# Moving the start of the row gathers, the last dots of one tile and its weighing across the end of a fused layer's front

## Chip, cores, metric

One core of a Trainium2 chip. The time is the device time of one execution in microseconds, the median over executions. The core has TensorE (PE, with its weight loads shown apart as PEld), VectorE (DVE), ScalarE (ACT), GpSimd (POOL) and SyncE (SP), each running its own stream of instructions in order; semaphores hold one engine until another, or a DMA, is done. DMAs are issued from the queues of SP, ACT and POOL and carried by 16 DMA engines. The granted clock that the profile shows for TensorE is a share of full speed, 1.00 at most.

## The reference, cut to what matters

One post-norm encoder layer over 1024 tokens of width 1024, float32. A projection feeds two mixers (forgetting attention and RWKV-7); their merge and a layer norm give x; then a PEER block adds, for each token and each of 8 heads, 16 experts out of 16384:

```python
q = (xb @ w_q).reshape(t, PEER_HEADS, 2, PEER_HALF)
s = jnp.einsum('thpd,hpkd->thpk', q, sub_keys)
top_s, top_i = lax.top_k(s, K)                       # K = 16 of 128, twice
...
best_s, best_pos = lax.top_k(cand_s.reshape(t, PEER_HEADS, K * K), K)
idx = jnp.take_along_axis(cand_i.reshape(t, PEER_HEADS, K * K), best_pos, axis=-1)
gate = jax.nn.softmax(best_s, axis=-1)
h = jax.nn.gelu(jnp.einsum('thkd,td->thk', u_table[idx], xb), approximate=False)
return jnp.einsum('thk,thkd->td', gate * h, v_table[idx])
```

So every token takes 128 rows of the table u (a dot with x each), a gelu, a gate, and a weighted sum of 128 rows of the table v. Then a second layer norm.

## The kernel before, in words

**Tiles.** The tokens are 8 tiles of 128. The *front* runs two halves of 512 tokens, each through `fox`, `rwkv_half`, `merge_half` and, at the end of the merge, `queries` (L1286): W_Q projections in sixteen column blocks, in four groups of four; each group's results are copied from PSUM to `q` on ACT (L1331) and scored against the keys `sk` (`scores`, called one group late), the scores are copied to `sc` (L1316) and stored from ACT's queue to the DRAM buffer `scd` (L1319).

**Experts two ways.** Tiles 3, 4 and 5 (`DENSE`) take all 16384 experts: their chosen experts and gates are turned into one-hot operands, multiplied on PE into a dense weight matrix, and u and v are read whole. Tiles 0, 1, 2, 6 (`GATHERED`) and 7 (`LAST`) gather. In `experts_in` (L1452) u's rows come one gather for a column of 128 indices (L1469, POOL) into a ring of places `g.keys`, and each is dotted with x on DVE (L1481, `tensor_tensor_reduce` into a column of `hh`); after 128 of them follow the gelu on ACT (L1486), the gate multiply on DVE (L1488) and a store to `cijd` in DRAM. The gate is loaded at the 65th dot, into a tile of its own. In the class `Rows`, v's rows are gathered in pairs (`gather`, L1852, POOL) and summed on PE (`pg<-vr,win`), with the weights placed by ACT into a window `win` of zeros.

**Background.** `topk` (L1346) and `experts_in` of all tiles form one background stream `g.B`, in the order k0, then each tile's experts mixed with the next tile's top-k: tile 0 with k1, tile 1 with k2, tile 2 with k3, then k4, k5, k6, tile 6 with k7, tile 7. Row sums form the stream `g.V`. Every matmul that goes through `mm` (L276) credits both with its modelled PE time multiplied by a rate; a dot costs 1.46 credits, a pair of rows 3. Rates by stage: `RATEP` for the three parts of the front, `RATEB` and `RATEV` later. `need(tag)` steps the stream until that part is done, whatever the credit.

**Order.** In the front PE's order is the program's and the other engines' is made when the program is built, by priorities, with background work high. In `dense_block` (from L1514) PE, POOL and DVE keep program order, and ACT and SP are ordered by priorities.

**The seam.** After the third group of projections `Rows.early` frees one of the `g.keys` places and loads into it tile 0's indices and weights and tile 3's selections (two POOL-queue DMAs). After the last projections `indices` turns both with six transposes on PE, copies them on ACT and makes the integer indices on DVE; then come the last scores. Then `begin(f"g2", "k3")` steps the background until tile 2's experts and tile 3's top-k are done; what is free of `g.keys` is lent as places and the first v rows are gathered. `vx` with `win` and the ring `vr`, `pp` with C (the dense weights) and, in `dense_block`, `bp` with the one-hot operands `ab` and `cT` are opened over the front's memory. A pool's first use waits for the release of everything that lay under it, unless the pool has `reuse_waits="tile"`, where each tile waits only for the tiles under itself.

**One-hot stage** (L1589 to L1630). k runs from −7 to 96, four tokens each. One-hots are made 3 steps ahead (`b` on DVE L1570, `a` on DVE L1576 or on ACT L1573, in turn), four products `v` go to PSUM, and two ACT copies move them: experts' first half to C (L1623), the rest to S (L1624), which is spilled every 8 steps (L1626, `cd<-S` on SP).

**Main loop** (L1730 on): for each j of 128, `usplit`, `hidden` (matmuls `b<-xh,uh`), `csplit` (a gelu on ACT, L1684, and multiplies with C), `vsplit` and `values`. u and v arrive by `uraw<-ut` and `vraw<-vt` on SP and are split into two fp32r parts by a cast on ACT and a subtraction (L293, L294). Ahead of the loop: two `usplit`, `hidden(0)`, `csplit(0)`, two steps of `g.V`, and two `vsplit`. Its pools are opened in the order `up` (raw u), `lp` (split parts, h), `rp` (raw v).

Of the kernel before, what the change touches and what calls it, by code (L numbers as in the profile page):

```python
# [23 lines left out]
BLEAD = 3  # L24
FIRST = 2.0
KRING = (5, 2)
TKW = (45.0, 56.25, 59.895)
TKI = 1
RATEP = (0.975, 0.975, 0.87)

# [373 lines left out]
def body(ctx, g):  # L404
# [36 lines left out]
    dve.tensor_copy(g.rank, g.iota[:, 0:16, None].to_broadcast([128, 16, 16]))  # L441
    g.scored, g.idx = set(), {}
    g.rows = Rows(g, GATHERED)
# [27 lines left out]
    with ExitStack() as fe:  # L471
        g.X = None
        setup = front_setup(g, fe, order)
        next(setup)
        for hf, (t0, n) in enumerate(PARTS):
            g.t0, g.n, g.cols = t0, n, slice(t0, t0 + n)
            with ExitStack() as hx:
                g.W.begin(hf, None if hf else hx.enter_context(tc.tile_pool(name="wr", bufs=1)))
                hp = hx.enter_context(tc.tile_pool(name="hp", bufs=1))
                kt = hp.tile([128, 4, n], F32, name="kt")  # L480
                more = [hp.tile([128, D], F32, name=f"g{i}") for i in range(KRING[1] if hf else 0)]
                g.keys.add(more)
                if g.X is None:
                    xload(g, hf, g.W._split)
                    next(setup)
                g.B.rate = RATEP[0]
                fox(g, hf, g.X)
                g.B.rate = RATEP[1]
                yr = rwkv_half(g, hf, g.X, kt) if g.stop != "fox" else None
                g.xs.close()  # L490
                g.X = None
                g.B.rate = RATEP[2]
                if g.stop not in ("fox", "rwkv"):
                    merge_half(g, hf, yr)
                g.keys.drop(more)
                g.B.busy = True
                while any(a is p for a in g.keys.alive.values() for p in more):
                    g.B._step()
                g.B.busy = False
    if g.stop:  # L500
        return
    g.rows.begin(f"g{SEL[-1] - 1}", f"k{DENSE[0]}")
    g.psB = ctx.enter_context(tc.tile_pool(name="psB", bufs=1, space=PSUM))
# [3 lines left out]
    g.spare, g.over = True, False  # L507
    g.rows.open()
    g.rows.places.add([g.vx.tile([128, D], F32, name=f"vr{i}") for i in range(RING)])
    g.V.add(g.rows.run())  # L510
    g.pp = ctx.enter_context(tc.tile_pool(name="pp", bufs=1))
# [774 lines left out]
def queries(g, hf, x1, rest, ps_):  # L1286
# [5 lines left out]
    with ExitStack() as fx:  # L1292
        qp = fx.enter_context(tc.tile_pool(name="qp", bufs=1))
        sk = qp.tile([128, 16, 128], F32, name="sk")
        sp.dma_start(sk, A["sk"])
        qs = {}

# [24 lines left out]
        for gr in range(4):  # L1322
# [12 lines left out]
            if gr == 1 and hf + 1 < len(PARTS):  # L1335
                xload(g, hf + 1)
            if gr == 2 and hf:
                g.rows.early()
        if hf:
            g.rows.indices(*[ps_.tile([128, 4, 128], F32, name=f"o{i}", bufs=2) for i in range(2)])  # L1340
        scores(*last)
# [112 lines left out]
def experts_in(g, tile_):  # L1454
# [17 lines left out]
    for k in range(128):  # L1472
        ahead()
        if k == 0:
            yield 1.0
            yield 1.0
        if k == 64:
            gate = P.tile([128, 128], F32, name="gate", bufs=1)
            sp.dma_start(gate, g.gated[tile_])
# [4 lines left out]
    if "hh" in g.dbg:  # L1484
        sp.dma_start(g.dbg["hh"][tile_ * 128:(tile_ + 1) * 128, :], hh)
    act.activation(hh, hh, AF.Gelu)  # L1486
    if tile_ != LAST:
        dve.tensor_mul(hh, hh, gate)  # L1488
        act.dma_start(g.cijd[tile_][:, 0, :], hh)
        yield 0.1  # L1490
        return
# [22 lines left out]
def dense_block(g, C):  # L1514
# [72 lines left out]
    lent = {1: g.rows.lent}  # L1587
    with tc.tile_pool(name="bp", bufs=BLEAD + 1) as bp, tc.tile_pool(name="cj", bufs=2) as cj:
        ab, pb = {}, {}  # L1589
        cT = bp.tile([128, 3, n - 128], F32, name="cT", bufs=1)  # L1590
        for k in range(-BLEAD - 4, n4 + 1):
# [13 lines left out]
            if 0 <= k < n4:  # L1605
                a, b = ab.pop(k)
                pb[k] = g.psV.tile([128, 4, 128], F32, name=f"v{k % 3}0")
                for u in range(4):
                    mm(g, pb[k][:, u, :], a[:, u, :], b[:, u, :], True, True)
            if k == n4 - XAT:  # L1610
                xp = zx.enter_context(tc.tile_pool(name="xp", bufs=1, side="right"))
# [21 lines left out]
    for q in range(UBUF):  # L1633
        uload(q)
    lp = lx.enter_context(tc.tile_pool(name="lp", bufs=2, reuse_waits="tile"))
    rp = lx.enter_context(tc.tile_pool(name="rp", bufs=VBUF, reuse_waits="tile"))
    for q in range(VBUF):
        load(q)

    def group(r):  # L1640
# [36 lines left out]
    def csplit(j):  # L1677

        if j < 128:
# [3 lines left out]
            h = lp.tile([128, n], F32, name="h")  # L1683
            act.activation(h, ph, AF.Gelu)  # L1684
            dve.tensor_mul(c, turned(h), c)
# [38 lines left out]
    g.V.busy = False  # L1724
    for q in range(2):
        vsplit(q)
    fin, old = iter(()), [p for j in range(LOOP, HALF - 7, 8) for i in range(nt) for p in parts(C, i, j, j + 8)]
# [34 lines left out]
class Rows:  # L1762
# [4 lines left out]
    def __init__(self, g, tiles):  # L1767
        self.g, self.tiles = g, tiles
        self.places, self.alive, self.meta, self.ng, self.pairs = Places(), [], {}, 0, False
        self.held = []  # L1770

    def open(self):

        self.win = self.g.vx.tile([128, 2, 159], F32, name="win")
        self.g.pool.memset(self.win, 0.0)

    def early(self):

        g = self.g
        kept, p = g.keys.all[:KRING[0]], None  # L1780
        g.B.busy = True
        while p is None:
            p = next((q for q in g.keys.free if any(q is a for a in kept)), None)
            if p is None:
                g.B._step()
        g.B.busy = False
        g.keys.free = [q for q in g.keys.free if q is not p]
        self.first = p
        g.pool.dma_start(p[:, 0:384].rearrange("p (a b) -> p a b", a=3), g.cijd[self.tiles[0]])
        g.B.need(f"k{DENSE[0]}")  # L1790
        g.pool.dma_start(p[:, 640:1024].rearrange("p (a b) -> p a b", a=3), g.cijd[DENSE[0]])

    def indices(self, pt, pd):

        g, p = self.g, self.first
        for j in range(3):
            g.pe.transpose(pd[:, j, :], p[:, 640 + 128 * j:768 + 128 * j], g.ident)
        cij = p[:, 0:384].rearrange("p (a b) -> p a b", a=3)
        for j in range(3):
            g.pe.transpose(pt[:, j, :], cij[:, j, :], g.ident)  # L1800
        self.meta[0] = self.turn(pt, cij, p[:, 384:512], p[:, 512:640].bitcast(I32))
        self.cT = p[:, 640:1024].rearrange("p (a b) -> p a b", a=3)
        g.act.copy(self.cT, pd[:, 0:3, :])
# [10 lines left out]
    def begin(self, *tags):  # L1814

        g = self.g
        for tag in tags:
            g.B.need(tag)
        self.lent = [g.keys.take() for _ in range(len(g.keys.free))]
        self.places.add(self.lent)  # L1820
        for _ in range(len(self.lent) // 2):
            self.gather()

# [21 lines left out]
    def gather(self):  # L1845
# [3 lines left out]
        for q in range(2):  # L1849
            place = self.places.take()  # L1850
            t = 64 * (k // 64) + 32 * q + k % 64 // 2
            g.pool.indirect_dma_start(out=place, out_offset=None, in_=g.A["v"], in_offset=bass.IndirectOffsetOnAxis(ap=self.meta[i][1][:, t:t + 1], axis=0))  # L1852
            self.alive.append(place)
        self.ng += 2

    def run(self):
        g, win = self.g, self.win
        prep = None
        for k in range(0, 128 * len(self.tiles), 2):
# [25 lines left out]
            if m == 31:  # L1885
# [4 lines left out]
                if s_:  # L1890
                    g.V.done.add(f"v{self.tiles[i]}")
                    if i == 0:
                        g.keys.give(self.first)
            del self.alive[:2]
# [135 lines left out]
```

## Time and profile before

| | us |
|---|---|
| median of 3 runs | 3493.19 (3491.34 to 3498.84) |
| profiled execution | 3488.81 |
| its span, first to last instruction | 3487.0 |
| busy PE | 3089.3 (89%) |
| busy DVE | 2376.6 (68%) |
| busy POOL | 1756.1 (50%) |
| busy ACT | 1140.0 (33%) |
| moved by DMA | 1132.22 MB, mean 325 GB/s |

The front ends about 1740 us into the span, the one-hot stage reaches to about 2180, the main loop to about 3455, and the last layer norms follow. Busy shares are averages over these stages. A row of the windows gives a stretch, its length, the busy time of PE, PEld, DVE, ACT and POOL with instruction counts, the granted clock, DMA's busy share (which can come out a little over 1) and GB/s. A row of a timeline gives the start, the busy time, the engine, the source line, the operation with output and inputs, and in brackets the idle time of the engine just before, with what ended it. A row of groups gives the count, the busy time and mean nanoseconds of one, then the idle time before them. DMA rows of the chain give the start and the time from issue to landing.

### The profile page before, as it was taken

The numbers are of one execution on the slowest core, as the hardware profiler recorded it, in microseconds if no ns is written. First come the engines' busy times: TensorE is split into PE (matmuls) and PEld (weight loads), VectorE is DVE, ScalarE is ACT, GpSimd is POOL, SyncE is SP. The second block draws the span as 40 slices with busy tenths as digits, with TensorE's granted clock in tenths as the row PEclk, the third lists the DMA queues.
The fourth block names the chain that finished last, engine by engine and source line by source line (L and its number), as shares of the span: only waits on it lengthen the run. The fifth ranks groups of instructions, "written<-read, shape, count | busy, mean of one in ns | idle before, by whom it ended". The sixth has DMA issues, their size and how long they took to land.

```text
span 3487.0 us, 54632 instructions
## 1 busy us (share of the span) xinstructions
PE 3089.3 (89%) x20141; PEld 2301.4 (66%) x20141; DVE 2376.6 (68%) x5489; ACT 1140.0 (33%) x2380; POOL 1756.1 (50%) x1430
## 2 busy tenths in 40 slices
PE   7899898999998878789777777999999999999996
PEld 5577776885566666567633332688887777777875
DVE  3234523358988898987479865687777767677776
ACT  3443223232432222111134443334333333333332
POOL 2032115325565456553464567555756566566761
PEclk9999999998998887989988989999999999999998
DMA  8373347889989778989998899999999999999995
GB/s 282 118 250 113 98 151 264 296 320 324 306 301 368 255 271 309 352 323 373 369 377 340 340 371 392 376 371 372 409 409 406 400 401 391 402 400 397 399 398 196
DMA packets 366876, 1132.22 MB, mean 325 GB/s; under 512 B 49456, under 2 KB 85936, under 8 KB 364816
## 3 DMA queue, kind: packets, MB, share of 16 engines
q0 software_dynamic: 184448, 671.56, 50.8%
q1 hardware_dynamic: 165760, 428.06, 33.7%
q10 hardware_dynamic: 16400, 29.11, 2.2%
q8 instruction: 158, 2.59, 0.3%
q14 instruction: 110, 0.90, 0.1%
HBM read 995.94 MB, written 132.64 MB: 324 GB/s over the span
## 4 chain that ended last, share of the span: by engine, by line
PE 47%; DVE 19%; DMA 16%; issue 7%; POOL 3%; ACT 2%; another core or an unknown queue 0%; SPq 0%; ACTq 0%; POOLq 0%; DVEq 0%
PE b L276 12%; PE v L276 10%; DMA uraw<-ut 8%; PE pj L276 7%; PE s L276 5%; PE o L276 5%; DVE g L1481 4%; PE pg L276 3%; DMA g<-u,idx 3%; PE S L276 2%; DVE ab L1570 1%; POOL g L1469 1%; DMA vr<-v,ve 1%; PE a L276 1%; DMA wl<-whd 1%
## 5 line engine op out<-in xcount | busy, mean ns | idle before, releaser
L1469 POOL DMA_INDIRECT g<-u,idx x569 | 685.3, 1204 | 609.0 <-DVE hh L1481 311.8
L1481 DVE CUSTOM_DVE_ANT_0 g<-g,ext 128x1024 f32<-128x1024 f32 x569 | 701.1, 1238 | 85.2 <-DMA g<-u,idx 66.8
L1852 POOL DMA_INDIRECT vr<-v,ve x285 | 338.1, 1186 | 174.0 <-PE pg L276 74.5
L276 PE MATMUL b<-xh,uh 128*128 128x384 f32 x1024 | 354.3, 346 | 41.0 <-ACT h L1684 39.7
L294 POOL TENSOR_TENSOR wl<-wraw,wh 128x1024 fp32r<-128x1024 f32 x63 | 152.7, 2424 | 436.7 <-ACT wh L293 337.2
L276 PE MATMUL b<-xl,uh 128*128 128x384 f32 x1024 | 352.1, 344 | 0.0
L276 PE MATMUL b<-xh,ul 128*128 128x384 f32 x1024 | 351.7, 343 | 0.1
L294 DVE TENSOR_TENSOR ul<-uraw,uh 128x512 fp32r<-128x512 f32 x256 | 176.0, 690 | 223.1 <-ACT uh L293 205.0
L276 PE MATMUL v<-vl,ch 128*128 128x512 f32 x768 | 301.9, 393 | 0.7 <-DVE vl L294 0.6
L276 PE MATMUL v<-vh,ch 128*128 128x512 f32 x768 | 301.1, 392 | 0.1
L276 PE MATMUL v<-vh,cl 128*128 128x512 f32 x768 | 300.9, 392 | 0.0
L276 PE MATMUL pj<-xh,wh 128*128 128x512 f32 x624 | 283.7, 455 | 13.9 <-ACT xh L293 7.1
L293 ACT CAST uh<-uraw 128x512 fp32r<-128x512 f32 x256 | 157.2, 620 | 410.2 <-PE b L276 210.0
L276 PE MATMUL pg<-vr,win 128*32 128x512 f32 x1364 | 243.2, 641 | 46.8 <-DMA vr<-v,ve 38.7
L276 PE MATMUL pj<-xl,wh 128*128 128x512 f32 x624 | 257.8, 413 | 2.4 <-DVE xl L294 2.4
L276 PE MATMUL pj<-xh,wl 128*128 128x512 f32 x624 | 257.5, 413 | 0.0
L276 PEld LDWEIGHTS b<-xh,uh 128*128 128x128 f32 x1024 | 196.3, 192 | 62.2 <-ACT h L1684 48.1
L276 PEld LDWEIGHTS v<-ab 128*128 128x128 f32 x768 | 111.1, 214 | 187.8 <-issue 113.4
L293 ACT CAST vh<-vraw 128x512 fp32r<-128x512 f32 x256 | 156.1, 618 | 162.1 <-PE v L276 115.5
L276 PEld LDWEIGHTS b<-xl,uh 128*128 128x128 f32 x1024 | 196.1, 192 | 15.2 <-issue 10.9
L276 PEld LDWEIGHTS b<-xh,ul 128*128 128x128 f32 x1024 | 195.9, 191 | 11.5 <-issue 9.8
L276 PE MATMUL v<-ab 128*128 128x128 f32 x768 | 139.8, 320 | 71.2 <-ACT S L1624 20.6
(395 smaller groups left out, 6555.2 us busy)
## 6 DMA issues: line engine op xcount, KB each, us to landing
uraw<-ut SPq DMA_DIRECT2D x128, 512.0 KB
vraw<-vt SPq DMA_DIRECT2D x128, 512.0 KB
wraw<-w SPq DMA_DIRECT2D x72, 512.0 KB
wh<-whd SPq DMA_DIRECT2D x72, 512.0 KB
wl<-whd SPq DMA_DIRECT2D x72, 512.0 KB
whd<-wh SPq DMA_DIRECT2D x71, 512.0 KB
whd<-wl SPq DMA_DIRECT2D x71, 512.0 KB
cd<-S SPq DMA_DIRECT2D x12, 1344.0 KB
```

The source lines that it names most:

```text
L276: g.pe.matmul(o, l, r, start=start, stop=stop_)
L293: g.act.copy(hi, src)
L294: (lo_eng or g.dve).tensor_sub(lo, src, hi.bitcast(F32))
L1469: pool.indirect_dma_start(out=place, out_offset=None, in_=A["uv"[n // 128]], in_offset=bass.IndirectOffsetOnAxis(ap=idx[:, n % 128:n % 128 ...
L1481: dve.tensor_tensor_reduce(out=gg, in0=gg, in1=xt, scale=1.0, scalar=0.0, op0=OP.mult, op1=OP.add, accum_out=hh[:, k:k + 1])
L1570: dve.tensor_scalar(b[:, u, :], g.iota, cT_[:, 2, t], cT_[:, 0, t], op0=OP.is_equal, op1=OP.mult)
L1852: g.pool.indirect_dma_start(out=place, out_offset=None, in_=g.A["v"], in_offset=bass.IndirectOffsetOnAxis(ap=self.meta[i][1][:, t:t + 1], ...
```

## The change

1. `RATEP[2]` 0.87 becomes 0.80; `KRING` (5, 2) becomes (6, 2), one more place for gathered rows for the whole front. `more`, the second half's two extra places, is dropped from the ring after the third group of projections.
2. `win` and a buffer of its own for what `early` loads (`p0`) move into the pool `g.gp`.
3. `early` runs at the start of the second `queries` and loads only tile 0's indices and weights, on ACT's queue. `indices` turns them in the first group. `coming` loads tile 3's selections after the third group (POOL's queue, after k3); `weights` turns them before the last scores.
4. `begin` asks for k3 alone. Three pairs of rows are gathered into `vr` places first, then the free `g.keys` places are lent and more pairs follow, ordered behind the first on POOL.
5. Tile 2's gelu, gate multiply and store become `weigh`, called in the one-hot stage once the dots are done and k is at least 4, with the gelu at that place in ACT's order.
6. In `experts_in` the gate is loaded at dot 126 and not 64, into the memory of the tile's indices (tile 7: of `t1`).
7. `bp` and `cj` get `reuse_waits="tile"`.
8. `rp` is opened ahead of `lp`; the casts of the first two `vsplit` are ordered behind the last gelu issued.
9. The scratch memory for POOL's DMA descriptors is 8192 bytes in place of the default 16384.

```diff
-KRING = (5, 2)
+KRING = (6, 2)
-RATEP = (0.975, 0.975, 0.87)
+RATEP = (0.975, 0.975, 0.8)
...
-    g.rows.begin(f"g{SEL[-1] - 1}", f"k{DENSE[0]}")
...
-    g.rows.open()
     g.rows.places.add([g.vx.tile([128, D], F32, name=f"vr{i}") for i in range(RING)])
+    g.rows.begin(f"k{DENSE[0]}")
...
         sp.dma_start(sk, A["sk"])
+        if hf:
+            g.rows.early()
...
+            if gr == 0 and hf:
+                g.rows.indices(ps_.tile([128, 4, 128], F32, name="o0", bufs=2))
             if gr == 2 and hf:
-                g.rows.early()
+                g.rows.coming()
+                g.keys.drop(g.more)
         if hf:
-            g.rows.indices(*[ps_.tile([128, 4, 128], F32, name=f"o{i}", bufs=2) for i in range(2)])
+            g.rows.weights(ps_.tile([128, 4, 128], F32, name="o0", bufs=2))
         scores(*last)
...
-        if k == 64:
-            gate = P.tile([128, 128], F32, name="gate", bufs=1)
+        if k == 126:
+            assert n >= 128
+            gate = g.tk.tile([128, 128], F32, name="t1") if tile_ == LAST else idx.bitcast(F32)
             sp.dma_start(gate, g.gated[tile_])
...
-    act.activation(hh, hh, AF.Gelu)
+    def weigh():
+        gelu = act.activation(hh, hh, AF.Gelu)
+        if tile_ == SEL[-1] - 1:
+            g.tc.keep_in_program_order(gelu)
+        if tile_ != LAST:
+            dve.tensor_mul(hh, hh, gate)
+            act.dma_start(g.cijd[tile_][:, 0, :], hh)
+    if tile_ == SEL[-1] - 1:
+        g.weigh = weigh
+        yield 0.1
+        return
+    weigh()
...
-    with tc.tile_pool(name="bp", bufs=BLEAD + 1) as bp, tc.tile_pool(name="cj", bufs=2) as cj:
+    with tc.tile_pool(name="bp", bufs=BLEAD + 1, reuse_waits="tile") as bp, tc.tile_pool(name="cj", bufs=2, reuse_waits="tile") as cj:
...
+            if g.weigh and k >= 4:
+                assert g.rows.ng < 128
+                g.weigh()
+                g.weigh = None
...
-    lp = lx.enter_context(tc.tile_pool(name="lp", bufs=2, reuse_waits="tile"))
     rp = lx.enter_context(tc.tile_pool(name="rp", bufs=VBUF, reuse_waits="tile"))
...
+    lp = lx.enter_context(tc.tile_pool(name="lp", bufs=2, reuse_waits="tile"))
...
-    for q in range(2):
-        vsplit(q)
+    with tc.issue_after(g.gelu.ins):
+        for q in range(2):
+            vsplit(q)
...
     def early(self):
...
-        g.B.need(f"k{DENSE[0]}")
-        g.pool.dma_start(p[:, 640:1024].rearrange("p (a b) -> p a b", a=3), g.cijd[DENSE[0]])
+        g.act.dma_start(self.first[:, 0:384].rearrange("p (a b) -> p a b", a=3), g.cijd[self.tiles[0]])
...
+    def coming(self):
+        g, p = self.g, self.first
+        g.B.need(f"k{DENSE[0]}")
+        g.pool.dma_start(p[:, 384:768].rearrange("p (a b) -> p a b", a=3), g.cijd[DENSE[0]])
...
-        self.lent = [g.keys.take() for _ in range(len(g.keys.free))]
+        for _ in range(len(self.places.free) // 2):
+            last = self.gather()
+        spare = len(g.keys.free)
+        self.lent = [g.keys.take() for _ in range(spare - (spare + len(self.places.free)) % 2)]
         self.places.add(self.lent)
-        for _ in range(len(self.lent) // 2):
-            self.gather()
+        with g.tc.issue_after(last.ins):
+            for _ in range(len(self.places.free) // 2):
+                self.gather()
...
-    nc = bacc.Bacc("TRN2", target_bir_lowering=False, num_devices=1)
+    nc = bacc.Bacc("TRN2", target_bir_lowering=False, num_devices=1, dynamic_dma_scratch_size=8192)
```

More of the change, by code (lines that the diff above doesn't have):

```diff
@@ L441, in body @@
     dve.tensor_copy(g.rank, g.iota[:, 0:16, None].to_broadcast([128, 16, 16]))
-    g.scored, g.idx = set(), {}
+    g.scored, g.idx, g.weigh = set(), {}, None
     g.rows = Rows(g, GATHERED)
@@ L482, in body @@
                 g.keys.add(more)
+                g.more = more
                 if g.X is None:
@@ L1485, in experts_in @@
         sp.dma_start(g.dbg["hh"][tile_ * 128:(tile_ + 1) * 128, :], hh)
-    act.activation(hh, hh, AF.Gelu)
+    def weigh():
[10 more added lines that the diff above has]
+    weigh()
     if tile_ != LAST:
-        dve.tensor_mul(hh, hh, gate)
-        act.dma_start(g.cijd[tile_][:, 0, :], hh)
         yield 0.1
@@ L1683, in csplit @@
             h = lp.tile([128, n], F32, name="h")
-            act.activation(h, ph, AF.Gelu)
+            g.gelu = act.activation(h, ph, AF.Gelu)
             dve.tensor_mul(c, turned(h), c)
@@ L1770, in __init__, with indices @@
         self.held = []
-    def open(self):
-        self.win = self.g.vx.tile([128, 2, 159], F32, name="win")
-        self.g.pool.memset(self.win, 0.0)
+        self.first = g.gp.tile([128, 768], F32, name="p0")
+        self.win = g.gp.tile([128, 2, 159], F32, name="win")
+        g.pool.memset(self.win, 0.0)
     def early(self):
         g = self.g
[L1780 to L1789, printed above, removed]
-        g.B.need(f"k{DENSE[0]}")
-        g.pool.dma_start(p[:, 640:1024].rearrange("p (a b) -> p a b", a=3), g.cijd[DENSE[0]])
-    def indices(self, pt, pd):
+        g.act.dma_start(self.first[:, 0:384].rearrange("p (a b) -> p a b", a=3), g.cijd[self.tiles[0]])
+    def indices(self, pt):
         g, p = self.g, self.first
-        for j in range(3):
-            g.pe.transpose(pd[:, j, :], p[:, 640 + 128 * j:768 + 128 * j], g.ident)
         cij = p[:, 0:384].rearrange("p (a b) -> p a b", a=3)
@@ L1800, in indices, with weights @@
             g.pe.transpose(pt[:, j, :], cij[:, j, :], g.ident)
-        self.meta[0] = self.turn(pt, cij, p[:, 384:512], p[:, 512:640].bitcast(I32))
-        self.cT = p[:, 640:1024].rearrange("p (a b) -> p a b", a=3)
+        self.meta[0] = self.turn(pt, cij, p[:, 0:128], p[:, 256:384].bitcast(I32))
+    def coming(self):
+        g, p = self.g, self.first
+        g.B.need(f"k{DENSE[0]}")
+        g.pool.dma_start(p[:, 384:768].rearrange("p (a b) -> p a b", a=3), g.cijd[DENSE[0]])
+    def weights(self, pd):
+        g, p = self.g, self.first
+        for j in range(3):
+            g.pe.transpose(pd[:, j, :], p[:, 384 + 128 * j:512 + 128 * j], g.ident)
+        self.cT = p[:, 384:768].rearrange("p (a b) -> p a b", a=3)
         g.act.copy(self.cT, pd[:, 0:3, :])
@@ L1851, in gather @@
             t = 64 * (k // 64) + 32 * q + k % 64 // 2
-            g.pool.indirect_dma_start(out=place, out_offset=None, in_=g.A["v"], in_offset=bass.IndirectOffsetOnAxis(ap=self.meta[i][1][:, t:t + 1], axis=0))
+            last = g.pool.indirect_dma_start(out=place, out_offset=None, in_=g.A["v"], in_offset=bass.IndirectOffsetOnAxis(ap=self.meta[i][1][:, t:t + 1], axis=0))
             self.alive.append(place)
         self.ng += 2
+        return last
     def run(self):
@@ L1891, in run @@
                     g.V.done.add(f"v{self.tiles[i]}")
-                    if i == 0:
-                        g.keys.give(self.first)
             del self.alive[:2]
```

## The prediction

> **What bounds the kernel now.** First the page's totals, its DMA row over 40 slices and the chain that ended last:
>
> ```profile
> span 3487.0 us, 54632 instructions
> DMA  8373347889989778989998899999999999999995
> PE 47%; DVE 19%; DMA 16%; issue 7%; POOL 3%; ACT 2%; another core or an unknown queue 0%; SPq 0%; ACTq 0%; POOLq 0%; DVEq 0%
> ```
>
> The profiled execution ran 3488.81 us (span 3487.0 and 1.8 outside it), 4.4 under the 3493.19 median of the runs; the sum is made against the former and 4.4 added at the end. TensorE carries half of the chain, and from the middle on DMA is full as well. Then the stretches around the seam that the change touches (start:end, us, busy of PE, PEld, DVE, ACT, POOL, then granted clock, DMA share, GB/s):
>
> ```profile
> 1697.00:1720.00 23.00, 21.32 (x115) 18.18 (x113) 13.97 (x23) 4.22 (x6) 11.51 (x12) 1.00 1.03 400
> 1720.00:1730.00 10.00, 0.27 (x1) 0.27 (x2) 7.79 (x15) 1.22 (x3) 2.22 (x3) 0.65 0.63 218
> 1730.00:1740.00 10.00, 5.03 (x30) 4.84 (x30) 0.52 (x2) 4.09 (x13) 5.83 (x7) 0.84 0.83 260
> 1740.00:1764.00 24.00, 9.92 (x47) 4.71 (x48) 6.08 (x21) 4.47 (x13) 15.88 (x17) 0.64 1.03 402
> 1764.00:2022.00 258.00, 190.40 (x1124) 90.46 (x1123) 230.10 (x1064) 118.02 (x388) 141.64 (x142) 0.85 0.91 343
> 2022.00:2178.00 156.00, 114.72 (x555) 45.41 (x554) 89.87 (x278) 54.03 (x179) 111.40 (x101) 0.90 1.01 393
> 2178.00:2202.00 24.00, 14.64 (x52) 7.36 (x53) 5.21 (x14) 7.17 (x15) 11.50 (x12) 0.69 1.02 411
> 2202.00:2670.00 468.00, 468.00 (x2511) 386.30 (x2511) 361.65 (x724) 179.39 (x359) 283.76 (x239) 1.00 1.01 388
> ```
>
> Up to 1718 the front projects, PE full. From 1720 to 1764 PE works 15.2 of 44 us. Then the one-hot stage: DVE sets its pace at first (230 of 258 us), DMA from 2022 on (1.01). From 2178 to 2202 PE works 14.6 of 24 us, and from 2202 the main loop holds it without a gap. Two holes, then, at the seams of the one-hot stage; what ends each stands in the timelines of PE, ACT and DVE (start, us, instruction, and in brackets the idle time before it and its releaser):
>
> ```profile
> 1729.73 5.30 PE L276 MATMUL o<-sk,q 128*128 128x128 f32 x30 [11.41 <-ACT q L1331]
> 1745.88 0.77 PE L276 MATMUL v<-ab 128*128 128x128 f32 x2 [10.85 <-DVE ab L1576]
> ...
> 2186.39 2.18 PE L276 MATMUL pg<-vr,win 128*32 128x512 f32 x8
> 2191.64 1.91 PE L276 MATMUL pg<-vr,win 128*32 128x512 f32 x2 [3.06 <-DMA vr<-v,ve]
> 2193.87 1.93 PE L276 MATMUL pg<-vr,win 128*32 128x512 f32 x6 [0.32 <-DMA vr<-v,ve]
> 2200.66 0.69 PE L276 MATMUL b<-xh,uh 128*128 128x384 f32 x1 [4.86 <-ACT h L1684]
> ```
> ```profile
> 1728.06 0.31 ACT L1486 ACTIVATE hh<-hh 128x128 f32<-128x128 f32 x1 [24.88 <-DVE hh L1481]
> 1729.09 1.56 ACT L1331 COPY q<-o 128x512 f32<-128x512 f32 x3 [0.72 <-DVE hh L1488]
> 1763.45 0.31 ACT L1623 COPY C<-v 128x176 f32<-128x176 f32 x1 [14.57 <-DMA C<-v,g]
> 2194.56 1.14 ACT L293 CAST vh<-vraw 128x512 fp32r<-128x512 f32 x2 [15.16 <-DMA vraw<-vt]
> 2198.82 1.28 ACT L1684 ACT_TABLE_LOAD   x1
> 2200.12 0.49 ACT L1684 ACTIVATE h<-b 128x384 f32<-128x384 f32 x1
> ```
> ```profile
> 1744.07 1.11 DVE L1570 TENSOR_SCALAR ab<-base,g 128x128 f32<-128x128 f32 x4 [12.00 <-DMA scd<-sc]
> 1745.10 0.68 DVE L1576 TENSOR_TENSOR ab<-base,g 128x512 f32<-128x512 f32 x1
> ...
> 1763.45 1.11 DVE L1570 TENSOR_SCALAR ab<-base,g 128x128 f32<-128x128 f32 x4 [13.85 <-remote]
> ```
>
> ACT stands 24.88 us at tile 2's gelu, which needs all 128 dots of that tile; the copies of the last three query projections are queued behind it, so PE waits 11.41 us for scores whose inputs are long in PSUM. The first one-hots then wait for the stores of those scores, and PE 10.85 more. A third hole follows, where DVE waits 13.85 us for something that the trace cannot name.
>
> **The change part by part, gain counted positive.** *Gelu moved* behind the fifth one-hot product: the copies go as soon as the projection ends.
>
> ```profile
> 1690.30 0.59 ACT L1331 COPY q<-o 128x512 f32<-128x512 f32 x1 [4.85 <-PE o L276]
> 1643.14 3.73 PE L276 MATMUL o<-sk,q 128*128 128x128 f32 x32
> ```
>
> Of 11.41 us one copy and its handover stay, 0.59 and some 0.3: +10.5. The scores then run without a long pause ahead of them, in the 3.73 us that 32 of them took at 1643 instead of 5.30 for 30: +1.5. *One-hot buffers that wait by tile*: they lie over the keys' half tiles and the queries, not over the scores' copies, so the last scores' matmuls free them, not the stores. What is left of 10.85 is one one-hot, 1.11 + 0.68 us, and a handover, 2 in all: +8.8. PE thus starts the stage at about 1725 instead of 1745.9. *The 13.85 us stall*: I know no cause, so it is taken to recur, 0. Its ends: all 13.85 gained, if the row gathers into C did it as the ACT row has it, and 10 lost, if the same gathers, now ahead of it, make it longer.
>
> *Dots moved into the one-hot stage.* The front's last rate falls from 0.87 to 0.80 credits per modelled PE us; by the cost model in the code the merge and the queries of the second half are 177.5 of those, so 12.4 credits, and at 1.46 a dot 8 dots of tile 2 are late. The dense stage runs them in program order on DVE, which paces it.
>
> ```profile
> L1481 DVE CUSTOM_DVE_ANT_0 g<-g,ext 128x1024 f32<-128x1024 f32 x384 | 475.9, 1248 | 76.9 <-DMA g<-u,idx 58.4 <-DMA cijd<-hh 9.1 <-issue 8.7
> L1570 DVE TENSOR_SCALAR ab<-base,cT 128x128 f32<-128x128 f32 x148 | 42.0, 361 | 0.5 <-issue 0.3 <-ACT cT L1560 0.2
> ```
>
> Eight by 1.248 are 10 us, the upper end if top-k falls behind by nothing. The credits are the same in number, so most dots put off steps of the next top-k to later, where DVE has room (362 of 468 us in the main loop); only that tile 4's must be done for the 25th one-hot forces some back: lower end 3. With the gate's load, now issued two dots before the end, DVE may stand a few us more, with the one-hots queued behind. I take 5: −5.
>
> *Row gathers first.* They begin when the indices are turned, with the last projections, and not after the gelu:
>
> ```profile
> 1721.20 0.94 POOL L1469 DMA_INDIRECT g<-u,idx  x1 [0.31 <-issue]
> 1732.34 0.95 POOL L1852 DMA_INDIRECT g<-v,g  x1 [9.82 <-DVE g L1811]
> L1852 POOL DMA_INDIRECT vr<-v,ve x285 | 338.1, 1186 | 174.0 <-PE pg L276 74.5
> ```
>
> POOL stands 9.82 us of that time. The new index load sits on ACT's queue, the three transposes, their copies and the two DVE steps go beside projections that PE is full of anyway: 0, and if that cover is gone, what the transposes take, under 1 us. The last u gathers of tile 2 come to stand behind 16 row gathers at about 1.25 us each on POOL, so until about 1740; the dots waiting for them come into the stage then, and their price is in the 5 above. *Scratch ring halved*: 0; if each gather took twice its 0.94, the first eight would come 8 us late. The Trainium skill, "SBUF — State Buffer", section "SBUF: two separate sides", has a VectorE operation in a two-port mode lock GpSimd out of writing a gather's descriptors, which would speak against more dots beside gathers; the gather at 1721.20 took its 0.94 us among dots end to end, so the sum leaves it at 0, where by the page it would be up to 10 us less.
>
> *End of the stage.* ACT casts V rows ahead of the first gelu, and those rows wait for the spill:
>
> ```profile
> 2178.38 9.14 DMA cd<-S
> 2187.54 6.94 DMA vraw<-vt
> ```
>
> The casts' 15.16 us wait then holds up the table load and the gelu that PE needs for its next group. In the change the casts come after that gelu, and the row buffers are laid out ahead of the split tiles, to lie over memory that is free earlier than the spilled tile. What is late next is PE's own work: two background steps that weigh gathered rows, in PE's order ahead of that group, the second waiting 3.06 us for its rows and ending at 2195.8. So of the hole PE's last 4.86 us go; the ends are 0 (DMA keeps the order of landings, and PE waits for V's rows a few matmuls later instead) and 9.5 (all up to 2191, where the rows have landed too). I take the row: +5.
>
> *Front.* One more place for gathered rows in the second half, against 58.4 us of DVE waits on them; 8% fewer dots there; the gate loads of tiles 0 and 1 later. From −17 (both gates uncovered, below) to +8; most rows say small: +2.
>
> *DMA must fit.* It stood empty 0.37 x 10 + 0.17 x 10 = 5.4 us from 1720 to 1740 and 0.09 x 258 = 23 us in the one-hot stage; later it has nothing free. So the gain fits, barely: I take 2 off.
>
> Sum: 10.5 + 1.5 + 8.8 − 5 + 0 + 5 + 2 − 2 = 20.8; 3488.8 − 20.8 = 3468.0 for a profile, and 3472 with 4.4 for the median.
>
> **Rivals.** *DMA takes the gain back*: the holes close, but the same bytes move at 1.01 share from 2022 to the end; only the 5.4 us of empty DMA are won, since the 9% of the one-hot stage are handovers that stay. 3493.2 − 5.4 = 3488. For it: the share row; against it: the main loop's first 468 us are bound by PE without a gap. The Trainium skill, "DMA: Bandwidth & Descriptors", section "Issuing engines are not separate DMA queues", speaks for this: transfers interleave on the same 16 engines whoever starts them, so that row gathers begun early would only push others back; the 1.03 at 1740 and 1.01 after 2022 agree, the 0.63 at 1720 does not.
>
> *The third hole goes too*: with the gathers 14 us earlier what DVE waits for has landed: 3472 − 13.85 = about 3458. For it: ACT's releaser is a row gather; against it: DVE's isn't named.
>
> *It doesn't do what it says*: if the first one-hots still lie over the scores' copies, 8.8 come back: about 3481.
>
> *Slower: gate loads hold DVE in the front.* Loaded at dot 126, a gate arrives after the last dot, and DVE, which bounds that stage, stands behind its multiply at tiles 0 and 1.
>
> ```profile
> 1775.65 9.20 DMA C<-cijd
> 1200.00:1300.00 100.00, 78.25 (x1000) 60.39 (x999) 95.34 (x254) 21.84 (x37) 55.15 (x46) 0.85 0.80 276
> ```
>
> A landing of 9.2 us twice is 18.4, decisive once no other DVE work is ahead of the multiply (DVE 95 of 100 us there); with DMA leaving only 5.4 of the gain, 3493.2 + 13 = 3506. Against it: the front's DVE order is made by a scheduler that can put other work ahead.
>
> **How the numbers follow.** Forecast 0.55, DMA takes it back 0.13, third hole gone 0.11, not as it says 0.11, slower 0.10. About 0.2%, 7 us, is what a measurement of this kernel can tell from no change: same is 3486 to 3500. Faster 0.55 + 0.11 + 0.11 = 0.77, same 0.13, slower 0.10. The forecast's own range, with the ends of the dots (3 to 10), the casts (0 to 9.5) and a front of −3 to +8, is 3458 to 3487: 2 + 4.5 + 6 better and the 2 of DMA, 5 + 5 + 5 worse. Below it, the third hole's case with some 8 of these is reached at 3450; above, the case of full DMA at 3488 with 3 for the front: 3491. What is left out is the slower case and the edges, 2 in 10.
>
> **What would show it.** In the profile after: PE's idle before the last 30 scores under 2 us, before the first one-hot product about 2; a row gather on POOL near 1718; dots among the one-hots on DVE, 8 of them, with waits on gathers or the gate of under 10 us together; the gelu of tile 2 without the 24.88; V's casts after the first gelu of the loop, PE's 4.86 us on ACT there gone; DMA's share in the one-hot stage near 0.97. Wrong if the one-hot stage, first product to last, grows by what the start gained, if DVE waits on a gate at tiles 0 and 1, or if POOL's gathers take longer than 1.19 us in the mean.

## The result, and the profile after

The changed kernel takes 3480.56 us in the median of 13 runs (3472.12 to 3491.77), and the kernel before took 3498.84 in the 13 beside them: a ratio of 0.995, 95% interval 0.9933 to 0.9967, so 17 us or 0.5% faster. 3472 had been forecast, inside 3450 to 3491. The profiled execution ran 3478.08 us, 10.7 under the one before. The page's totals and its chain:

```profile
span 3476.3 us, 54642 instructions
PE 52%; DVE 19%; DMA 12%; issue 6%; POOL 2%; ACT 2%; another core or an unknown queue 1%; SPq 0%; ACTq 0%; DVEq 0%; POOLq 0%
```

The same stretches as before:

```profile
1720.00:1730.00 10.00, 10.00 (x59) 4.45 (x52) 6.72 (x18) 4.46 (x17) 8.17 (x7) 0.88 1.03 409
1730.00:1740.00 10.00, 8.87 (x49) 3.47 (x50) 2.26 (x6) 3.06 (x10) 7.84 (x8) 1.00 0.99 381
1740.00:1764.00 24.00, 15.20 (x40) 4.79 (x34) 4.10 (x9) 4.12 (x14) 16.33 (x17) 0.70 0.98 371
1764.00:2022.00 258.00, 181.91 (x1084) 86.36 (x1084) 227.63 (x1056) 116.78 (x372) 131.00 (x133) 0.86 0.90 337
2022.00:2178.00 156.00, 111.72 (x520) 46.35 (x520) 81.46 (x249) 48.31 (x160) 109.34 (x101) 0.88 0.98 374
2178.00:2202.00 24.00, 17.93 (x80) 11.91 (x81) 12.89 (x30) 8.49 (x19) 9.66 (x10) 0.79 1.03 409
```

The seam of 1720 to 1740, where PE worked 5.3 us, now holds 18.9 us of PE and DMA is full in it. What stands there in the timelines of PE, ACT, DVE, POOL and SP:

```profile
1705.63 3.74 PE L276 MATMUL o<-sk,q 128*128 128x128 f32 x32
1711.55 0.46 PE L276 MATMUL v<-ab 128*128 128x128 f32 x2 [2.18 <-DVE ab L1593]
...
1771.69 0.77 PE L276 MATMUL v<-ab 128*128 128x128 f32 x2 [10.10 <-DVE ab L1587]
...
2183.41 1.91 PE L276 MATMUL pg<-vr,win 128*32 128x512 f32 x2 [5.91 <-DMA vr<-v,ve]
```
```profile
1759.92 0.19 ACT L1903 COPY win<-p 128x2 f32<-128x2 f32 x1 [9.16 <-remote]
...
1765.99 0.31 ACT L1494 ACTIVATE hh<-hh 128x128 f32<-128x128 f32 x1
...
2185.18 0.49 ACT L1705 ACTIVATE h<-b 128x384 f32<-128x384 f32 x1
2185.56 1.13 ACT L293 CAST vh<-vraw 128x512 fp32r<-128x512 f32 x2
```
```profile
1736.69 1.23 DVE L1487 CUSTOM_DVE_ANT_0 g<-g,ext 128x1024 f32<-128x1024 f32 x1 [8.11 <-DMA g<-u,idx]
1743.32 1.23 DVE L1487 CUSTOM_DVE_ANT_0 g<-g,ext 128x1024 f32<-128x1024 f32 x1 [4.36 <-DMA g<-u,idx]
1747.78 1.23 DVE L1487 CUSTOM_DVE_ANT_0 g<-g,ext 128x1024 f32<-128x1024 f32 x1 [1.60 <-DMA g<-u,idx]
1770.99 0.29 DVE L1498 TENSOR_TENSOR hh<-hh,idx 128x128 f32<-128x128 f32 x1 [21.98 <-DMA idx<-gated]
```
```profile
1706.89 0.94 POOL L1875 DMA_INDIRECT vr<-v,p  x1 [0.30 <-issue]
1730.94 0.95 POOL L1474 DMA_INDIRECT g<-u,idx  x1 [0.30 <-issue]
```
```profile
1761.56 0.32 SPq L1647 DMA_DIRECT2D cd<-S  x1
1762.22 0.30 SPq L1485 DMA_DIRECT2D idx<-gated  x1
```

The first hole is gone: the scores follow the projections at once and the first one-hot product 2.18 us after its predecessors. Two waits have taken its place, both on DVE among the one-hots. The last three dots of tile 2 wait 14.1 us for their rows, whose gathers come 24 us and more behind the first row gather on POOL. The gate multiply then waits 21.98 us, for two things. The gate's load may only overwrite the indices once the last gather that reads them has landed, and SP issues it behind the first spill of S, at 1762. And the multiply needs the gelu, which stands on ACT behind copies that wait themselves (one 9.16 us, for something that the trace cannot name) and ends at 1766.30. So only the last 4.7 us of the 21.98 belong to the gate's load alone. The one-hots behind that multiply are late, and PE 10.10 us with them.

To see where the 10.7 us are won and lost, the span is cut at events that both kernels have (starts in the timelines: first dot; first `o<-wh,mh` of the second half's merge; end of the last projection; first `v<-ab`; first and ninth `b<-xh,uh`; last one), here with all kernels of the experiments below, one profiled execution each. Executions of one kernel differ by some 10 to 30 us (e10 ran 3462 to 3491), so one row is one sample:

```
                 start   first dot  merge to   proj. to   one-hot   hidden 1  main   span
                 to dot  to merge   last proj. one-hots   stage     to 9      loop
before           797.1   757.3      163.0      28.5       433.0     21.8      1249.5 3487.0
after            792.6   747.5      165.4       6.0       459.1     17.2      1251.7 3476.3
e1  gate         798.0   750.2      165.3       6.9       444.7     17.1      1250.9 3469.8
e2  rate 0.87    800.8   751.0      181.3       5.8       445.9     18.0      1249.5 3489.1
e3  pool waits   793.0   746.6      163.3      16.0       438.6     18.6      1251.5 3464.4
e4  end          794.8   750.4      164.4       5.8       455.5     20.3      1248.3 3476.3
after, again     796.8   737.9      162.9       5.9       429.7     16.9      1252.6 3439.5
e5  place alone  789.1   733.3      163.3      27.9       408.4     21.7      1254.3 3434.9
e6  gate, 0.87   792.2   742.0      167.5       8.6       413.3     17.8      1251.5 3429.7
e7  gate, pool   791.9   735.4      164.7      15.5       419.4     17.1      1250.0 3430.8
e9  gate, 0.83   796.9   749.5      167.7       6.1       431.1     20.6      1250.2 3458.9
e10 gate again   791.6   747.0      165.3       7.0       446.7     17.1      1249.2 3460.6
e11 no place     797.4   758.2      163.4      11.2       442.3     19.3      1255.2 3483.8
e12 gate, 0.87   794.6   755.5      166.0       9.3       443.5     19.4      1255.4 3480.4
```

From the last hidden matmul to the end it is 36.7 to 36.9 us everywhere. After against before: −4.5, −9.8, +2.4, −22.5, +26.1, −4.6, +2.2. The first is scatter (789 to 801 in kernels alike up to there). So in these two executions the front, the start of the one-hot stage and its end gained 34.5 us between them, and the one-hot stage gave 26.1 back.

### The profile page after: what moved, and what is told of

Read it like the earlier page. It is cut to its first block, busy times and chain, and to the rows that moved or that the text cites. A ratio compares the mean times of both kernels' runs of the same rounds, so it can differ in the third digit from the quotient of the medians.

```text
span 3476.3 us, 54642 instructions
## 1 busy us (share of the span) xinstructions
PE 3087.4 (89%) x20141; PEld 2291.9 (66%) x20141; DVE 2375.7 (68%) x5489; ACT 1141.6 (33%) x2380; POOL 1760.3 (51%) x1429
## 4 chain that ended last, share of the span: by engine, by line
PE 52%; DVE 19%; DMA 12%; issue 6%; POOL 2%; ACT 2%; another core or an unknown queue 1%; SPq 0%; ACTq 0%; DVEq 0%; POOLq 0%
PE b L276 12%; PE v L276 12%; PE pj L276 7%; PE o L276 6%; DVE g L1487 5%; PE s L276 5%; PE pg L276 5%; DMA uraw<-ut 4%; DMA vr<-v,ve 3%; PE S L276 2%; DMA g<-u,idx 2%; DVE ab L1587 1%; DMA wl<-whd 1%; PE po L276 1%
## 5 line engine op out<-in xcount | busy, mean ns | idle before, releaser
L1474 POOL DMA_INDIRECT g<-u,idx x577 | 696.8, 1208 | 622.3 <-DVE hh L1487 313.5
L1487 DVE CUSTOM_DVE_ANT_0 g<-g,ext 128x1024 f32<-128x1024 f32 x577 | 710.7, 1239 | 98.9 <-DMA g<-u,idx 80.1
L276 PE MATMUL b<-xh,uh 128*128 128x384 f32 x1024 | 352.2, 344 | 36.4 <-ACT h L1705 32.8
L276 PE MATMUL pg<-vr,win 128*32 128x512 f32 x1420 | 276.3, 650 | 57.5 <-DMA vr<-v,ve 40.2
L276 PEld LDWEIGHTS b<-xh,ul 128*128 128x128 f32 x1024 | 194.8, 190 | 14.2 <-issue 9.6
L294 DVE TENSOR_TENSOR vl<-vraw,vh 128x512 fp32r<-128x512 f32 x256 | 176.1, 691 | 37.8 <-ACT vh L293 24.3
```

Of the source, the lines that this page charges most:

```text
L276: g.pe.matmul(o, l, r, start=start, stop=stop_)
L294: (lo_eng or g.dve).tensor_sub(lo, src, hi.bitcast(F32))
L1474: pool.indirect_dma_start(out=place, out_offset=None, in_=A["uv"[n // 128]], in_offset=bass.IndirectOffsetOnAxis(ap=idx[:, n % 128:n % 128 ...
L1487: dve.tensor_tensor_reduce(out=gg, in0=gg, in1=xt, scale=1.0, scalar=0.0, op0=OP.mult, op1=OP.add, accum_out=hh[:, k:k + 1])
```

## The experiments

The kernels of a group (e1 to e4; the changed kernel again with e5 to e7; e9 to e12) ran beside the kernel before on one chip; the chips differ (before took 3496, 3452 and 3498 us in the three groups), so ratios are compared within a group.

**e1, the gate early.** The gate of tile 2 goes into a part of p0 that is free once the indices are turned.

```diff
+        if k == 126 and tile_ == SEL[-1] - 1:
+            gate = g.rows.first[:, 128:256]
-        if k == 126:
+        elif k == 126:
...
     def coming(self):
+        g.sp.dma_start(p[:, 128:256], g.gated[SEL[-1] - 1])
```

> The changed kernel, but tile 2's gate is loaded from SP's queue with the last group of projections into a free part of p0, and no longer at dot 126 into the index tile. Theory A: the 21.98 us that DVE stands at tile 2's gate multiply, with the one-hots queued behind it, are most of what the one-hot stage lost, because the load stands on SP's queue behind the first spill. Then DVE waits under 3 us there, the copy to C of k = 8 comes some 18 us earlier than its 1766, the main loop's second group of hidden matmuls some 13 to 18 us earlier than its 2188, and the time is 0.990 to 0.992 of before. Rival B: the stage is paced by top-k of tile 4 and by DMA; the wait goes, k = 8 comes earlier, but by k = 28 (1865) the lead is gone and the time stays at 0.994 to 0.996.

3472.63 us, ratio 0.9934 (0.9909 to 0.9959). DVE no longer waits for the gate. But it still stood twice ahead of k = 8, here with the gelu on ACT:

```profile
1754.01 1.12 DVE L1589 TENSOR_SCALAR ab<-base,p 128x128 f32<-128x128 f32 x4 [11.77 <-remote]
1769.77 0.29 DVE L1500 TENSOR_TENSOR hh<-hh,p 128x128 f32<-128x128 f32 x1 [7.96 <-issue]
```
```profile
1769.42 0.31 ACT L1496 ACTIVATE hh<-hh 128x128 f32<-128x128 f32 x1
```

The first lies in a stretch in which PE goes on one instruction at a time with nothing to wait for (the third hole of the prediction). The second is the gelu's: the multiply starts when it ends. Theory A had put the whole 21.98 us down to the gate, but most of it was the gelu's in the changed kernel too. k = 8 came at 1770, not near 1748. The stage was 14.4 us shorter; the time lies between theory A and B and can't be told from the changed kernel's 0.995.

**e2, the rate back** (`RATEP[2]` 0.87).

> The changed kernel with RATEP[2] back at 0.87, so that the dots of tile 2 run in the front as before. Theory A: the front ended 12 us earlier because 7 dots (8.7 us) were taken out of a DVE that paces the merge and queries; then the last projection ends near 1715 to 1717 again and not at 1705, no dots stand among the one-hots, and the gate, loaded two dots before the end, has landed by the time it is needed: the time is 0.993 to 0.997. Rival B: the front's gain came from the added ring place; the last projection still ends near 1705 and the time is 0.989 to 0.992.

3492.51 us, ratio 0.9987 (0.9967 to 1.0007): nearly all of the gain gone, by a mechanism that neither theory had. The timelines of PE and SP:

```profile
1724.77 0.80 PE L276 MATMUL o<-xh,wh 128*128 128x512 f32 x1 [14.93 <-DMA wh<-whd]
```
```profile
1720.80 0.32 SPq L1485 DMA_DIRECT2D idx<-gated  x1
1721.23 0.37 SPq L324 DMA_DIRECT2D wh<-whd  x1
```

The gate's load waits on SP for the gathers that read the indices, and the weights of the last projection stand behind it. At the lower rate of the changed kernel the load comes after the projections, at 1762.

**e3, waits by pool** (`bp` and `cj` without `reuse_waits="tile"`).

> The changed kernel with the pools bp and cj waiting as before, for the release of everything under them. Theory A: PE's idle time ahead of the first one-hot product is 9 to 11 us again and not 2.18, and since DVE then stands for the gate anyway, only part of it reaches the end: 0.995 to 0.998. Rival B: all 8.8 us reach the end: 0.997 to 0.999. Rival C: the stores of the scores land while the row gathers hold DMA, so the wait is longer than before, 12 us or more, and the time 0.998 or above.

3473.99 us, ratio 0.9948 (0.9928 to 0.9967), level with the changed kernel's 0.995. The wait was there and did not reach the end; the stage itself came out 20.5 us shorter, in a profiled execution that is the quickest of its 12. The gate multiply waits 17.62 us here too, to the end of the gelu at 1763.64, with no part of it the gate's:

```profile
1718.88 0.77 PE L276 MATMUL v<-ab 128*128 128x128 f32 x2 [12.10 <-issue]
```
```profile
1763.68 0.29 DVE L1498 TENSOR_TENSOR hh<-hh,idx 128x128 f32<-128x128 f32 x1 [17.62 <-issue]
```

**e4, the end of the stage undone** (`lp` opened ahead of `rp`, the casts of V free).

> The changed kernel with lp opened ahead of rp again and the first casts of V free to go ahead of the first gelu. Theory A: that part was worth what the second group of hidden matmuls gained on the first, 21.7 us apart before and 17.3 after, so about 4.5 us: the two groups are 20 to 23 us apart again and the time is 0.996 to 0.997. Rival B: DMA's landings set that seam and the distance stays at 17 to 19 us, the time at 0.994 to 0.996.

3482.41 us, ratio 0.996 (0.9941 to 0.9978). The casts stand ahead of the gelu again and PE waits as it did before the change:

```profile
2191.15 0.69 PE L276 MATMUL b<-xh,uh 128*128 128x384 f32 x1 [4.97 <-ACT h L1705]
```

20.3 us between the two groups and not 17.2: 3 of the 4.6 us. In time, 0.996 can't be told from 0.995.

**The changed kernel again.**

> The changed kernel once more, beside the three below: 0.993 to 0.997 of before. Its second profile tells which of the stalls recur: if PE's slow steps near 1742 to 1760, one instruction each 0.7 us with nothing to wait for, belong to the program, they come again within 5 us of the same one-hots; if not, they move or go.

3439.97 us, ratio 0.9965 (0.9951 to 0.9979). PE's slow steps of 1742 to 1760 did not come; of DVE's two waits the rows' kept 14.2 us and the gate multiply's had 6.62:

```profile
1728.51 1.22 DVE L1487 CUSTOM_DVE_ANT_0 g<-g,ext 128x1024 f32<-128x1024 f32 x1 [8.51 <-DMA g<-u,idx]
1747.14 0.29 DVE L1498 TENSOR_TENSOR hh<-hh,idx 128x128 f32<-128x128 f32 x1 [6.62 <-DMA idx<-gated]
```

**e5, the ring place alone**, on the kernel before.

```diff
-KRING = (5, 2)
+KRING = (6, 2)
...
-    nc = bacc.Bacc("TRN2", target_bir_lowering=False, num_devices=1)
+    nc = bacc.Bacc("TRN2", target_bir_lowering=False, num_devices=1, dynamic_dma_scratch_size=8192)
```

> The kernel before with one thing of the change: one more ring place for gathered rows (KRING 6, 2), paid for by halved descriptor memory. Theory A: from the first dot to the last projection the changed kernel needs 913 us where before needs 920, with 747 to 751 against 757 already gone by at the merge, where the rate is the same, so the place is worth all of it: here too 913 and a time of 0.997 to 0.999. Rival B: the halved descriptor memory costs as much or the place hides nothing: 920 and 0.999 to 1.001.

3443.34 us, ratio 0.9978 (0.9966 to 0.999), where the whole change gave 0.9965. That is theory A's time. From the first dot to the last projection it takes 896.6 us where the changed kernel takes 900.8 on this chip, both far from the 913 and 920 of the first chip. So the place, with the smaller descriptor memory, is worth 0.22% (0.1 to 0.34). Its one-hot stage is 408.4 us beside 429.7 of the changed kernel on this chip: 21 us are lost there with no slow steps of PE in either.

**e6, gate early and rate 0.87.**

> The changed kernel with the gate loaded early into p0 and RATEP[2] back at 0.87. With the rate alone put back, the gate's load at dot 126 held SP's queue until the last gathers had landed, the weights of the last projections came late behind it, PE stood 14.93 us for them, and the time was 0.9987. Theory A: that queue was the whole loss; now the projections run through, the dots end with them, and the time is 0.991 to 0.995, as good as with the lower rate. Rival B: 7 dots in a DVE-paced front cost what they cost, 4 to 9 us more than with the rate of 0.80 (0.9934): 0.995 to 0.997.

3430.47 us, ratio 0.9942 (0.9921 to 0.9963), the best of this group: theory A, though the interval reaches into B. The projections run through (167.5 us and not 181.3), and the stage takes 413.3 us.

**e7, gate early, waits by pool.**

> The changed kernel with the gate loaded early into p0 and bp and cj waiting by pool. With the waits alone put back the time did not move (0.9948 against 0.995), PE standing 12.10 us ahead of the first one-hot product. Theory A: that was hidden behind DVE's wait for the gate; with the gate early it shows, 4 to 9 us: 0.995 to 0.997 where the early gate alone gave 0.9934. Rival B: the start of the one-hot stage isn't what its end hangs on; the time stays at 0.992 to 0.994.

3437.99 us, ratio 0.9964 (0.995 to 0.9978), level with the changed kernel's 0.9965. Against it the start is 9.6 us longer and the stage 10.3 shorter. Since the gate alone was not in this group, its 0.9934 of another chip can't be set beside this, so theory A is not excluded in time.

**e9, gate early and rate 0.83.**

> The changed kernel with the gate loaded early into p0 and RATEP[2] at 0.83: 3 dots of tile 2 are left for the one-hot stage, not 7, and all gathers of u's rows are issued ahead of the row gathers. Theory A: the price of the late dots is not their own time but that the gathers of the last three stand on POOL's queue and on DMA behind the row gathers, DVE waiting 14 to 22 us for them (22.3 of group g<-u,idx in the second profile of the changed kernel); here that wait is under 6 us, from the first one-hot product to the first hidden matmul 410 to 418 us go by, and the time is 0.991 to 0.994. Rival B: the dots' own time and the top-k steps put off set the stage, so 3 dots cost 3 sevenths: 0.994 to 0.996.

3459.12 us, ratio 0.9884 (0.9859 to 0.9909): 1.2% faster than before, the best kernel of all, and quicker than either theory had it. On POOL the last gather of u's rows is issued ahead of the first row gather, and none of the dots among the one-hots waits:

```profile
1715.40 0.94 POOL L1474 DMA_INDIRECT g<-u,idx  x1 [0.31 <-PE o L276]
1716.65 0.94 POOL L1878 DMA_INDIRECT vr<-v,p  x1 [0.30 <-issue]
```
```profile
1723.68 1.21 DVE L1489 CUSTOM_DVE_ANT_0 g<-g,ext 128x1024 f32<-128x1024 f32 x1
1733.48 1.22 DVE L1489 CUSTOM_DVE_ANT_0 g<-g,ext 128x1024 f32<-128x1024 f32 x1
1752.20 1.21 DVE L1489 CUSTOM_DVE_ANT_0 g<-g,ext 128x1024 f32<-128x1024 f32 x1
```

The stage took 431.1 us and not 410 to 418; PE's slow steps were there.

**e10, gate early and rate 0.80, in the same group.**

> The changed kernel with the gate loaded early into p0 and the rate of 0.80, beside the two rates above it. Theory A: the gate alone takes away the smaller wait only, 7 to 22 us by chip and execution; DVE's wait for the last three u rows stays at 14 to 22 us, and the time is 0.994 to 0.9965, behind both other rates. Rival B: the gate is all: 0.992 to 0.994, level with them.

3476.33 us, ratio 0.9939 (0.9918 to 0.996): 17 us behind 0.83, so not level with it, but level with 0.87 (e12): neither theory as it stands, and the number lies on the border of their ranges. Its profiled execution, with a span of 3460.6, is its quickest, and in it the dots did not wait for rows either, where theory A had 14 to 22 us. So the times show that 0.83 is better here, and the profiles do not show in which wait.

**e11, the change without the place** (`KRING` (5, 2)).

> The changed kernel with KRING back at (5, 2): the seam's parts without the ring place. Theory A: the place alone gave 0.9978 where the whole change gave 0.9965, so what remains of the change is worth 0.1 to 0.2%: 0.998 to 1.0. Rival B: the parts do not add, and the seam alone gives 0.995 to 0.997.

3486.87 us, ratio 0.9976 (0.996 to 0.9993). From the first dot to the merge it takes 758.2 us again, and all the seam's parts together are worth 0.24%, between the two theories. With e5's 0.22% they make 0.46%, where the whole change gave 0.5% on one chip and 0.35% on another. The intervals are too wide to say more than that the parts may add.

**e12, gate early and rate 0.87, in the same group.**

> The changed kernel with the gate loaded early and RATEP[2] at 0.87, once more for the comparison of three rates on one chip. Theory A: no dot and no gather is left, the front is 4 to 6 us longer than at 0.83: 0.993 to 0.996, not ahead of 0.83. Rival B: any dot in the one-hot stage costs more than in the front: 0.991 to 0.994 and ahead of both other rates.

3478.53 us, ratio 0.994 (0.9919 to 0.9962): as before for this kernel, and theory A. The rate of 0.83 is ahead of both neighbours, by intervals that do not meet, on this one chip.

## Why the prediction was right, and where it was not

The time lies in the range. A gain of 20.8 us was forecast, 17 was measured between the medians and 10.7 between the two profiled executions. But the mechanism was right in part only, and luck had its share: the range was 41 us wide, and half of the gain came from elsewhere. The seam's parts, 18.8 us of the forecast, are worth about 8 (e11: 0.24%); the ring place, priced at 2 us with all else in the front, about 8 as well (e5: 0.22%).

*Start of the one-hot stage*: 10.5 + 1.5 + 8.8 = 20.8 forecast, 22.5 measured (28.5 to 6.0). Right, and its parts too: PE's wait for the copies is nothing, the scores take 3.74 us, and e3 and e7 put the waits by tile at 10.0 and 9.6. **The step that failed** is the next one, that this start carries through to the end for a price of 5 us. In e3 and e7 the 10 us that the start lost came back from the stage, and the time did not move beyond its interval of some 0.2%. The stage grew by 26.1, more than the start had gained: the first of the prediction's own signs of being wrong.

*Dots in the one-hot stage*: −5, with an upper end of 10, for a stage that grew by 26.1. There are 7 of them, not 8. The term priced their own 1.248 us and had most of the top-k steps that they put off done later, where DVE has room. These steps were done in the stage, as the windows from the first one-hot product to k = 8 and from k = 16 to 28 show (starts of ACT's copies `C<-v`), before and after:

```profile
1745.90:1791.50 45.60, 34.62 (x176) 15.02 (x177) 30.85 (x147) 16.52 (x54) 28.11 (x29) 0.77 0.99 388
1832.40:1866.90 34.50, 29.42 (x180) 14.49 (x181) 32.81 (x133) 22.63 (x74) 14.36 (x14) 0.81 0.93 359
```
```profile
1711.50:1766.20 54.70, 40.13 (x160) 14.94 (x160) 19.09 (x50) 16.47 (x52) 40.73 (x38) 0.76 1.00 386
1811.80:1864.80 53.00, 33.71 (x207) 16.67 (x207) 47.78 (x216) 26.50 (x82) 23.33 (x24) 0.84 0.88 320
```

To k = 8, DVE is busy 19 of 54.7 us, with no top-k step done; from 16 to 28 it works off what was put off (216 instructions and 47.8 us, against 133 and 32.8), since tile 4's must be ready. The same measure in every profile, from the copy of k = 16 to that of k = 32, shows what this costs (late dots are those of tile 2 that stand among the one-hots):

| late dots | kernels | us from k = 16 to k = 32 |
|---|---|---|
| 0 | before, e2, e5, e6, e12 | 51.8 to 54.0 |
| 3 | e9 | 61.0 |
| 7 | after (twice), e1, e3, e4, e7, e10, e11 | 62.9 to 72.7 |

In e1 and e10 no late dot waited for its row, and they take 65.6 and 67.3 us. So this part is the work put off and not the waits. It is 12.8 of the 26.1 us (65.9 against 53.1). The other 13.7 fall ahead of k = 16 (100.2 against 86.5), where DVE's two waits and PE's slow steps lie; how these share them is not shown. From k = 32 on the two kernels take the same 293 us.

The gate's load had been put at "a few us more", and that holds. The multiply's waits read 21.98 and 6.62 us in the two profiles, but the gelu ended only 4.7 and 5.1 us ahead of it; the rest is the wait for the gelu, for which the sum had no term.

*Front*: +2 forecast, 7.4 measured (9.8 and −2.4). Groups of dots in the front, before and after:

```profile
L1481 DVE CUSTOM_DVE_ANT_0 g<-g,ext 128x1024 f32<-128x1024 f32 x376 | 466.1, 1248 | 76.2 <-DMA g<-u,idx 58.1 <-DMA cijd<-hh 9.1 <-issue 8.7
```
```profile
L1487 DVE CUSTOM_DVE_ANT_0 g<-g,ext 128x1024 f32<-128x1024 f32 x377 | 467.5, 1250 | 67.4 <-DMA g<-u,idx 57.9 <-DMA cijd<-hh 8.1 <-issue 1.0
```

DVE's idle time falls by 8.8 us; e5, with the place alone, has 66.0 of it, and e11, without the place, 75.4. The prediction looked at the 58 us on gathers, which did not move; the 8.7 on "issue" went. The lower rate, which the term also counted, wins nothing that shows: but for e2, merge to last projection is 163 to 168 us at 0.80, 0.83 and 0.87.

*End of the stage*: +5 forecast, 4.6 measured, with the releaser that was named: e4 brings the 4.97 us on ACT back. It is not always as much: with the change in place the two groups are 16.9 to 18.6 us apart in most kernels, but 19.3 to 20.6 in e9, e11 and e12; why is not shown.

*Third hole*: taken to recur, and it did here. In the kernel before PE goes one instruction at a time from 1753 to 1765, while DVE stands its 13.85 us. It does not belong to these instructions: none of the four kernels of the second group has a stretch of 8 us of it there, nor has e3, and in the third group it is there again. What makes PE take 0.7 us and more for each instruction stays open.

*DMA must fit*: from the first one-hot product to the first hidden matmul DMA's share was 0.95 before and 0.94 after, not 0.97. *Of the rivals*, slower by gate loads in the front is out: from the 128th dot to the multiply it takes 3.5 us in both kernels at tile 0 (1081.5 to 1085.0, 1075.3 to 1078.8), at tile 1 3.0 and 4.4 us. The mechanism was real at tile 2 instead, and through SP's queue (e2), which the rival did not name. DMA taking it all back is out in time (5.4 us, where the interval is 11 to 23); that the first one-hots wait as before is out, by PE's 2.18 us.

*Gathers beside dots*: 0, read off the gather at 1721.20 with its 0.94 us. That row was a lucky one: it began 0.13 us before its dot ended. A gather that begins earlier in a dot ends 0.8 us after that dot, as this one of the kernel before, and its dot:

```profile
1716.46 1.89 POOL L1469 DMA_INDIRECT g<-u,idx  x1 [0.30 <-issue]
```
```profile
1716.31 1.23 DVE L1481 CUSTOM_DVE_ANT_0 g<-g,ext 128x1024 f32<-128x1024 f32 x1 [1.06 <-DMA g<-u,idx]
```

Of 268 gathers there that begin 0.15 us or more before the end of a dot, 257 end 0.79 to 0.83 us after it; the 166 that run with no DVE instruction beside them take 0.94 us in the median and never more than 1.15. The 0 holds in size all the same: the gathers of u's rows take 1.20 us in the mean before and 1.21 after. The Trainium skill, "SBUF — State Buffer", section "SBUF: two separate sides", has a VectorE operation in a two-port mode lock GpSimd out; the trace agrees in the lock, and no run shows in which mode the dot runs.

*Transfers pushed back*: the late rows landed within 5.8 to 6.3 us of their gathers' issue (1730.94 to 1736.69, the first of them). What made them late was their place among the row gathers on POOL, and the gate's load stood behind the spill on SP. The Trainium skill, "DMA: Bandwidth & Descriptors", section "Issuing engines are not separate DMA queues", has transfers interleave whoever starts them; DMA's share of 0.98 to 1.03 from 1720 to 1764 agrees that the engines were full, but the two delays shown came from the order of issue.

## What to carry to other kernels

When work is moved past a seam, price what it puts off in its new place, before its own duration: 7 dots of 1.25 us made the stretch from k = 16 to 32 some 9 to 21 us longer, because the steps that they put off were due there. Where a wait has two releasers, look at the one that would have come next: the gelu alone held the multiply for 17 of the 22 us that the profile puts down to the gate. A load into memory that others still read holds up its whole queue (14.93 us of PE in e2), so give it memory that is free. A rate of 0.83 with the gate loaded early gave 1.2% where the change gave 0.5% and 0.35% on other chips; it leaves 3 late dots and issues the last gathers of u's rows ahead of the row gathers, and which of the two counts is not shown.

## What the runs showed of the hardware that was not expected

The same program took 3496, 3452 and 3498 us on the chips of the three groups, 1.3% apart, more than any part of this change. In all profiles of the first and the third group but e3, and in none of the second, PE went through some 11 to 20 us early in the one-hot stage at 0.7 to 2.8 us an instruction, with no semaphore to wait for that the profile shows, while DMA's share was about 1.0; here in the kernel before:

```profile
1757.83 0.37 PE L276 MATMUL v<-ab 128*128 128x128 f32 x1 [2.53 <-issue]
1760.62 0.37 PE L276 MATMUL v<-ab 128*128 128x128 f32 x1 [2.43 <-issue]
```
